# A hybrid decoder block on one core: state-space outputs turned round and double-buffered, q, k, v moved behind them, attention with its scores one block ahead

## The chip, the cores and the metric

The kernel runs on one core of a Trainium2 chip, as one program. The metric is device time in microseconds (us), the median of several executions; lower is better. The engines are named as in the profile: PE is TensorE (matmuls; PEld is its weight load, one for each matmul), DVE is VectorE, ACT is ScalarE, POOL is GpSimd, and SP is the engine that issues most of the DMAs. "q" behind a name (SPq, ACTq) is that engine's instruction queue. PEclk is the clock that TensorE was granted, as a share of its full 2.4 GHz; there are two levels, 1.0 and 0.5.

## The reference

One layer over 512 tokens of width 2048, all in float32:

```python
h = modulate(rmsnorm(x, g_mix), shift1, scale1)          # shift, scale, gate: silu(c) @ w_ada + b_ada
q, k, v, u, gate_logits = split(h @ w_in + b_in)         # 1024 + 256 + 256 + 1024 + 2 * 2048 columns
y_attn = sliding_window_attention(rope(q), rope(k), v, sinks) @ w_attn_branch
y_ssm = s5_ssm(u, ...) @ w_ssm_branch
merged = sigmoid(gate0) * y_attn + sigmoid(gate1) * y_ssm
x = x + gate1 * (merged @ w_out)
x = x + gate2 * peer(modulate(rmsnorm(x, g_ffn), shift2, scale2), ...)   # product-key experts
return rmsnorm(x, g_final)
```

Attention has 16 query heads over 4 key heads, a window of 128 and blocks of 128 tokens. The state-space branch has 64 groups of 16 channels with 64 complex states each: a scan over time, outputs `C x + D u`, then gelu and a gated linear unit. The change touches the layer from the u projection to the attention branch; the expert part behind it, which takes the larger half of the time, is as before.

## The kernel before

Activations lie channel-major (128 channels by 512 tokens a tile). A large product keeps float32 accuracy by splitting both factors into a rounded part and a rest and adding three matmuls (`product`, L201 to L203). One **projection** is 128 output channels over 2048 inputs: 48 matmuls of 512 columns, two weight loads of 512 KB on SP's queue, a cast on ACT (L185) and a subtraction on DVE (L187) for each. `w_in` has 52 projections: 8 for u in the head, and 44 others, of which 12 are q, k and v and 32 are gate logits. Each projection of gate logits also issues two pieces of the adaLN product, each a 512 KB load and one DVE instruction (L140).

The order is this. **Head** (L408 to L466): the first adaLN columns, the norm, and the eight u projections in five cuts of the contraction. In the second and third cut (c of 1 and 2) the rest of the weights is taken on POOL (L437). POOL also prepares the state-space part there: constants, powers (L356) and the rotation tables `rc`, `rs` (L372 to L380, doubling from 1 to 64 columns in six steps), which SP then stores (L527 to L529).

**State-space slices** (`ssm_slice`, L545 to L674): eight slices of eight groups. A slice has four steps: (1) POOL forms the tables `mt`, `cl_r`, `cl_i`; (2) PE transposes `mt` (L581), forms the small kernel `km` (L590, L591), which goes through DRAM and comes back as `intra` (L598 to L602), and turns u (L613); (3) PE forms the chunk inputs (L623), and DVE rotates them, scans over 64 chunks and rotates back (L629 to L652); (4) PE forms the outputs (L661 to L663): for each of eight groups three products of a 128-column stationary table with 64 moving columns, x being the moving side. ACT copies them out and they go to `y_d` in pieces of 64 elements. Between the steps the loop takes one projection from `dense()` at a time: 16 in all here, the 12 of q, k, v first. Most tiles of a slice have one buffer.

**Attention** (`attend`, L688 to L733): 16 blocks, four query blocks by four key heads, query block outermost. Each has scores (L699), a masked softmax on DVE, ACT and POOL, four or eight transposes (L721) and the product with v (L726). One projection follows in program order after the first half of each block, 16 in all. The 12 that are left run behind it (L739). Then come the attention branch (`w_ab`, L764), with the gelu of `y_d` on ACT beside it (L759 to L762), the gated linear unit, and the rest.

Program order is not the order on the chip. The framework plans every engine's instruction order ahead of time on a simulated timeline (L1300): of the instructions that are ready there it takes the earliest in the program; weight loads have a head start (L172). On the chip each engine, and SP's queue, then keeps that order and waits where an operand is late. `issue_after(ins)` plans a block's instructions of that engine behind `ins`. Every fp32 matmul outside `product` shows as two rows in the trace.

Of the kernel before, what the change touches and what calls it, by code (L numbers as in the profile page):

```python
# [18 lines left out]
TT = 4  # L19
# [40 lines left out]
def hybrid_block(tc, I, out, dbg=None):  # L60
# [311 lines left out]
    nc.gpsimd.memset(rc[:, :, 0:1], 1.0)  # L372
    nc.gpsimd.memset(rs[:, :, 0:1], 0.0)
    w = 1
    while w < 64:
        ub, vb = (z[:, :, None].to_broadcast([128, PAIRS, w]) for z in (ur, ui))
        cmul(rc[:, :, w:2 * w], rs[:, :, w:2 * w], rc[:, :, 0:w], rs[:, :, 0:w], ub, vb, ra[:, :, 0:w])
        cmul(vr, vi, ur, ui, ur, ui, t0)
        ur, ui, vr, vi = vr, vi, ur, ui
        w *= 2  # L380
# [49 lines left out]
    def head_product(c):  # L430
        k0, n = HEAD_CUTS[c]
        if c == 0:
            head.extend(mm_tile() if i % 2 else aux_tile() for i in range(8))
        for i in range(8):
            h, l = split_weights(I["w_in"][12 + i][k0 // 8][:, k0 % 8 * 128:(k0 % 8 + n) * 128], n,
                                 nc.gpsimd.tensor_tensor if c in (1, 2) else tt)
            for k in range(n):  # L437
                kk = k0 + k
                nc.tensor.matmul(head[i], h[:, k], h_hi[:, kk], start=(kk == 0), stop=False)
                nc.tensor.matmul(head[i], h[:, k], h_lo[:, kk], start=False, stop=False)  # L440
                nc.tensor.matmul(head[i], l[:, k], h_hi[:, kk], start=False, stop=(kk == KT - 1))
            yield
# [15 lines left out]
    y_d = dr.tile([1024, 8, 64], F32, name="y_d")  # L458
# [8 lines left out]

    ap_ = pool("ap", "left")
    qr = ap_.tile([128, 8, T], F32, name="qr")
    kr = ap_.tile([128, 2, T], F32, name="kr")  # L470
    vv = ap_.tile([128, TT, 256], F32, name="vv")
    rp = pool("rp", "left")
    rcos = rp.tile([128, T], F32, name="rcos")
    rsin = rp.tile([128, T], F32, name="rsin")
    posi = tmp.tile([128, T], I32, name="t0", tag="t0")
    ang = row("ev")
    nc.sync.dma_start(posi, I["positions"][None, :].to_broadcast([128, T]))
    nc.vector.tensor_copy(ang, posi)
    ts(ang, ang, freq, None, op0=OP.mult)
    reduce_angle(ang, rcos)  # L480
    sin_cos(rsin, rcos, ang)
    ts(rsin, rsin, sgn, None, op0=OP.mult)
# [22 lines left out]
    def dense():  # L505
        jobs = [(8 + i, rope, kr[:, i]) for i in range(2)]
        jobs += [(10 + i, value, vv[:, :, i * 128:(i + 1) * 128]) for i in range(2)]
        jobs += [(i, rope, qr[:, i]) for i in range(8)]
        last = None
        for m, finish, dst in jobs:  # L510
            o = projected(m)
            if last:
                last[0](*last[1:])
            last = finish, dst, o
            yield
        for i in range(32):
            o = projected(20 + i, 1)
            nc.scalar.dma_start(sg_d[i], o)
            if last:
                last[0](*last[1:])  # L520
                last = None
            yield

    dense_work = dense()


    with tc.issue_after(loads[-1]):  # L527
        for i, t_ in enumerate((rc, rs)):
            nc.sync.dma_start(rot_d[:, :, i], t_.rearrange("p (a b) c -> p a b c", a=8))  # L529
# [5 lines left out]
    with tc.issue_after(loads[-1]):  # L535
        nc.sync.dma_start(bass.AP(tensor=km_d.tensor, offset=km_d[0].offset + 128, ap=[[240, 128], [30720, 8], [1, 112]]),
                            zero[:, None, :].to_broadcast([128, 8, 112]))
# [7 lines left out]
    def ssm_slice(s):  # L545
# [21 lines left out]
        cl_r, cl_i = tl("cl_r", [128, 4, 16, 8]), tl("cl_i", [128, 4, 16, 8])  # L567
# [9 lines left out]
        for mt, name in zip(mts, ("mi_r", "mi_i")):  # L577
            dst = tl(name, [128, 4, 128])
# [20 lines left out]
        iraw, intra = tl("iraw", [128, 8, 128]), tl("intra", [128, 8, 16, 8])  # L599
# [3 lines left out]
        rot = tl("rot", [128, 2, 256])  # L603
# [6 lines left out]
        u = tl("uc", [128, 8, 64])  # L610
# [3 lines left out]
        uj = tl("uj", [128, 8, 64])  # L614
# [12 lines left out]
        ta = tl("t2", [128, 512])[:, 0:256]  # L627
        w_r, w_i = (tl("mt", [128, 4, 16, 8], 2).rearrange("p a h j -> p (a h j)")[:, 0:256] for _ in range(2))
# [11 lines left out]
        x_r, x_i = tl("x_r", [128, 4, 64]), tl("x_i", [128, 4, 64])  # L640
# [13 lines left out]
        y = tl("uc", [128, 8, 64])  # L654
        for two in range(2):
            p = aux_tile()
            rows = slice(two * 64, two * 64 + 64)
            for a in range(4):
                g = 2 * a + two
                o = p[:, a * 64:(a + 1) * 64]  # L660
                nc.tensor.matmul(o, cl_r[rows, a].rearrange("p h j -> p (h j)"), x_r[rows, a], start=True, stop=False)  # L661
                nc.tensor.matmul(o, cl_i[rows, a].rearrange("p h j -> p (h j)"), x_i[rows, a], start=False, stop=False)
                nc.tensor.matmul(o, intra[:, 4 * two + a].rearrange("p h j -> p (h j)"), uj[:, g], start=False, stop=True)  # L663
            nc.scalar.copy(y[:, two::2], p[:, 0:256].rearrange("p (a c) -> p a c", a=4))
        nc.scalar.dma_start(chunked_ap(y_d), y)

    slices = [ssm_slice(s) for s in range(8)]
    next(slices[0])
    for s in range(8):
        for _ in slices[s]:  # L670
            next(dense_work)
        if s < 7:
            next(slices[s + 1])
    close(ss)  # L674
    close(sp)
    close(rp)
# [11 lines left out]
    def attend(b, n):  # L688
# [7 lines left out]
        for r2 in range(2):  # L696
            p = aux_tile().rearrange("p (a c) -> p a c", a=2)
            for r in range(2):
                nc.tensor.matmul(p[:, r, 0:wd], qr[rows, np_ * 4 + r2 * 2 + r, b * 128:(b + 1) * 128],  # L699
                                 kr[rows, np_, k0:k0 + wd], start=True, stop=True)  # L700
            stt(sv[:, 2 * r2:2 * r2 + 2], p[:, :, 0:wd], 0.125, mk[:, None, :].to_broadcast([128, 2, wd]),
                op0=OP.mult, op1=OP.add)
# [11 lines left out]
        yield  # L714
# [3 lines left out]
        for kc in range(nk):  # L718
            p = aux_tile()
            for r in range(4):  # L720
                nc.tensor.transpose(p[:, r * 128:(r + 1) * 128], sc[:, r, kc * 128:(kc + 1) * 128], ident)  # L721
            pt = aw.tile([128, 512], F32, name="pt", tag="pt", bufs=3)
            nc.scalar.copy(pt, p)
            pts.append(pt)
# [5 lines left out]
    for b in range(TT):  # L730
        for n in range(4):
            for _ in attend(b, n):
                next(dense_work)  # L733
    close(aw)
    close(ap_)
# [495 lines left out]

def shape_constants():
# [17 lines left out]
def device_inputs(x):  # L1250
# [5 lines left out]
    b_in = np.concatenate([l["b_in"][:1024][qo], l["b_in"][1024:]])  # L1256
    d = {
# [8 lines left out]
                                                     l["b_glu"])], axis=1),  # L1266
# [3 lines left out]
        "w_sb": chunked(l["w_ssm_branch"]),  # L1270
        "w_glu": chunked(l["w_glu"]),
# [33 lines left out]
```

## Time and profile before

| | us |
|---|---|
| median of 3 runs | 3866.27 (3858.65 to 3869.51) |
| profiled execution, its own time | 3862.01 |
| its span, first to last instruction | 3860.2 |
| mean granted clock of TensorE | 0.953 |

| stretch of the span, us | what runs |
|---|---|
| 0 to 206 | head |
| 206 to 558 | eight state-space slices, 16 projections and the start of the next |
| 558 to 901 | attention blocks, and projections |
| 901 to 931 | the last projections of gate logits |
| 931 to 1021 | attention branch |
| 1021 to 3860 | gated linear unit, merge, output product, experts, last norm |

A row of the timeline has the start, the time taken, the engine, the line and the operation, out<-in, the shape, how many were merged, and in brackets how long the engine sat idle before it and what released it. A row of the waits says who waited for whom, in total us, how many times, and the longest. A row of the stretches has each engine's busy time (and instructions), the granted clock, the share of the DMA engines and GB/s. A busy PE need not be at its peak, since matmuls overlap.

### The profile page before, as it was taken

The numbers are of one execution on the slowest core, as the hardware profiler recorded it, in microseconds if no ns is written. First come the engines' busy times: TensorE is split into PE (matmuls) and PEld (weight loads), VectorE is DVE, ScalarE is ACT, GpSimd is POOL, SyncE is SP. The second block draws the span as 40 slices with busy tenths as digits, with TensorE's granted clock in tenths as the row PEclk, the third lists the DMA queues.
The fourth block names the chain that finished last, engine by engine and source line by source line (L and its number), as shares of the span: only waits on it lengthen the run. The fifth ranks groups of instructions, "written<-read, shape, count | busy, mean of one in ns | idle before, by whom it ended". The sixth has DMA issues, their size and how long they took to land.

```text
span 3860.2 us, 51341 instructions
## 1 busy us (share of the span) xinstructions
PE 3572.5 (93%) x20045; PEld 3242.9 (84%) x20045; DVE 2757.2 (71%) x3948; ACT 1295.9 (34%) x1790; POOL 1006.0 (26%) x851
## 2 busy tenths in 40 slices
PE   7699999999999988887399999999999999998997
PEld 3477777777788888787389999999999999998997
DVE  7644445556863389999887888888867888857844
ACT  3232223334443332345323223333333233333323
POOL 7644520010000245255322212222202122212102
PEclk8889889999999999999599999999999999999999
DMA  8543345447954322267788899999976999958943
GB/s 294 195 154 87 115 147 178 166 161 290 330 168 161 126 64 74 83 245 289 270 324 327 337 336 348 345 343 353 347 251 246 334 342 344 340 179 290 327 128 113
DMA packets 274104, 921.60 MB, mean 239 GB/s; under 512 B 35394, under 2 KB 92866, under 8 KB 229956
## 3 DMA queue, kind: packets, MB, share of 16 engines
q1 hardware_dynamic: 204260, 533.91, 39.8%
q0 software_dynamic: 50048, 344.55, 24.5%
q10 hardware_dynamic: 19552, 39.85, 2.7%
q8 instruction: 157, 2.57, 0.3%
q14 instruction: 87, 0.71, 0.1%
HBM read 871.03 MB, written 47.12 MB: 238 GB/s over the span
## 4 chain that ended last, share of the span: by engine, by line
PE 64%; DVE 13%; issue 10%; DMA 7%; POOL 2%; ACT 1%; DVEq 0%; POOLq 0%; SPq 0%; ACTq 0%
PE mm L203 13%; PE mm L201 13%; PE mm L202 13%; PE aux L1187 6%; PE aux L1186 6%; PE aux L1185 6%; DVE wlo L187 2%; DMA rows<-in_up_rows,pick 1%; DMA rows<-in_down_rows,pick 1%; DMA gt<-g_d 1%; DMA raw<-in_up 1%; DVE rows L1016 1%; POOL rows L1010 1%; DVE cand L932 1%; DVE o L1089 1%
## 5 line engine op out<-in xcount | busy, mean ns | idle before, releaser
L185 ACT CAST whi<-raw 128x1024 fp32r<-128x1024 f32 (+2 forms) x744 | 759.3, 1022 | 1736.1 <-PE mm L202 811.2
L187 DVE TENSOR_TENSOR wlo<-raw,whi 128x1024 fp32r<-128x1024 f32 (+2 forms) x696 | 868.2, 1248 | 435.4 <-ACT whi L185 403.8
L203 PE MATMUL mm<-h_hi,wlo 128*128 128x352 f32 (+1 forms) x2752 | 955.5, 347 | 41.8 <-DVE wlo L187 41.6
L201 PE MATMUL mm<-h_hi,whi 128*128 128x352 f32 (+1 forms) x2752 | 952.2, 346 | 8.1 <-ACT whi L185 8.1
L202 PE MATMUL mm<-h_lo,whi 128*128 128x352 f32 (+1 forms) x2752 | 949.1, 345 | 0.0
L1185 PE MATMUL aux<-wh,whi 128*128 128x352 f32 x2048 | 667.7, 326 | 39.4 <-ACT wh L191 22.4
L1187 PE MATMUL aux<-wh,wlo 128*128 128x352 f32 x2048 | 669.8, 328 | 27.2 <-DVE wlo L187 27.1
L1186 PE MATMUL aux<-wl,whi 128*128 128x352 f32 x2048 | 667.9, 326 | 2.3 <-DVE wl L192 2.3
L203 PEld LDWEIGHTS mm<-h_hi,wlo 128*128 128x128 f32 x2752 | 525.9, 191 | 79.8 <-DVE wlo L187 50.1
L201 PEld LDWEIGHTS mm<-h_hi,whi 128*128 128x128 f32 x2752 | 525.7, 191 | 40.6 <-ACT whi L185 9.7
L202 PEld LDWEIGHTS mm<-h_lo,whi 128*128 128x128 f32 x2752 | 527.1, 192 | 32.0 <-issue 4.4
L1185 PEld LDWEIGHTS aux<-wh,whi 128*128 128x128 f32 x2048 | 390.7, 191 | 45.9 <-ACT whi L185 23.3
L1187 PEld LDWEIGHTS aux<-wh,wlo 128*128 128x128 f32 x2048 | 390.4, 191 | 35.1 <-DVE wlo L187 34.7
L1186 PEld LDWEIGHTS aux<-wl,whi 128*128 128x128 f32 x2048 | 390.3, 191 | 3.4 <-DVE wl L192 3.4
L1016 DVE SCALAR_TENSOR_TENSOR rows<-rows,hrow 128x2048 f32<-128x2048 f32 x160 | 370.3, 2316 | 18.8 <-DMA rows<-in_down_rows,pick 18.2
L140 DVE SCALAR_TENSOR_TENSOR adaw<-adaw,cb 128x1024 f32<-128x1024 f32 x176 | 227.3, 1298 | 146.5 <-DMA adaw<-in_w_ada 146.4
L1010 POOL DMA_INDIRECT rows<-in_up_rows,pick x128 | 151.7, 1185 | 577.2 <-DVE rows L1016 479.3
L1027 DVE SCALAR_TENSOR_TENSOR yrow<-rows,fit,yrow 128x2048 f32<-128x2048 f32 x127 | 297.8, 2345 | 4.1 <-DMA rows<-in_up_rows,pick 4.1
L1010 POOL DMA_INDIRECT rows<-in_down_rows,pick x128 | 151.8, 1186 | 525.4 <-DVE yrow L1027 291.6
L1188 DVE SCALAR_TENSOR_TENSOR x<-aux,mod,x 128x352 f32<-128x352 f32 x256 | 148.6, 581 | 181.2 <-PE aux L1187 180.8
L213 POOL TENSOR_TENSOR rstd<-rstd,t 128x512 f32<-128x512 f32 (+2 forms) x42 | 50.7, 1207 | 661.7 <-ACT t L211 661.0
L187 POOL TENSOR_TENSOR wlo<-raw,whi 128x1024 fp32r<-128x1024 f32 (+1 forms) x48 | 105.9, 2211 | 115.4 <-ACT whi L185 114.0
(431 smaller groups left out, 4696.1 us busy)
## 6 DMA issues: line engine op xcount, KB each, us to landing
raw<-in_down SPq DMA_DIRECT2D x256, 512.0 KB
raw<-in_up SPq DMA_DIRECT2D x256, 512.0 KB
adaw<-in_w_ada SPq DMA_DIRECT2D x192, 512.0 KB
raw<-in_w_in SPq DMA_DIRECT2D x88, 512.0 KB
g_d<-stg ACTq DMA_DIRECT2D x22, 1024.0 KB
gt<-g_d SPq DMA_DIRECT2D x16, 1408.0 KB
raw<-in_w_out SPq DMA_DIRECT2D x32, 512.0 KB
raw<-in_w_query SPq DMA_DIRECT2D x32, 512.0 KB
```

Source lines behind the costliest of these rows:

```text
L140: stt(w, w, 1.0, cb[:, half], op0=OP.mult, op1=OP.mult, accum_out=part[:, half:half + 1])
L185: nc.scalar.copy(h, r)
L187: sub(l, r, h.bitcast(F32), op=OP.subtract)
L201: nc.tensor.matmul(p, h[:, k], (xh[kk] if isinstance(xh, list) else xh[:, kk]), start=first, stop=False)
L202: nc.tensor.matmul(p, h[:, k], (xl[kk] if isinstance(xl, list) else xl[:, kk]), start=False, stop=False)
L203: nc.tensor.matmul(p, l[:, k], (xh[kk] if isinstance(xh, list) else xh[:, kk]), start=False, stop=last)
L1010: nc.gpsimd.indirect_dma_start(out=r.rearrange("p k c -> p (k c)"), out_offset=None, in_=I[table], in_offset=bass.IndirectOffsetOnAxis(ap= ...
L1016: stt(r, r, 1.0, hrow, op0=OP.mult, op1=OP.mult, accum_out=f[:, n:n + 1])
L1027: stt(y, r, f[:, n:n + 1], y, op0=OP.mult, op1=OP.add)
L1185: nc.tensor.matmul(p, h[:, j], WH[j], start=(j == 0), stop=False)
L1186: nc.tensor.matmul(p, h[:, j], WL[j], start=False, stop=False)
L1187: nc.tensor.matmul(p, l[:, j], WH[j], start=False, stop=(j == GI - 1))
```

## The change

Six edits, of which the last three only follow from the others.

- The rotation tables become a function, called on POOL behind the last POOL subtraction of the head's third cut; their stores, and a clear of `km_d`, move from SP's queue to POOL's.
- The slices come first, with the projections of gate logits 0 to 15 between their steps. Most tiles of a slice get two buffers (`w_r`, `w_i` their own), and step 1 runs two slices ahead, step 2 one.
- Outputs are turned round: x and u are stationary (64 columns), the tables move (128 columns). Two groups share the 128 output rows, one in each half. ACT copies, 16 small products with the identity turn the result back, ACT applies gelu, and `y_d` is stored as rows of 512.
- q, k, v are grouped by pairs of key heads. Seven of their projections run between the slices and attention.
- Attention has the key head outermost. Scores of the next block are issued first, then one or two projections whose PE work is planned behind those scores, then the rest of the block; the 21 projections that are left all lie there. `pt` has two buffers instead of three.
- `z` is loaded straight from `y_d`; the rows of `w_glu`, `w_ssm_branch` and `b_glu` are put in the new channel order on the host.

```diff
-    loads = []
+    loads, subs = [], []
...
-        sub(l, r, h.bitcast(F32), op=OP.subtract)
+        subs.append(sub(l, r, h.bitcast(F32), op=OP.subtract).ins)
...
+    def rotations(ur, ui, vr, vi):
...
+        for i, t_ in enumerate((rc, rs)):
+            nc.gpsimd.dma_start(rot_d[:, :, i], t_.rearrange("p (a b) c -> p a b c", a=8))
...
+            if c == 2 and i == 7:
+
+                with tc.issue_after(subs[-1]):
+                    rotations(ur, ui, vr, vi)
             yield
...
+    dense_work = gate_logits(range(16))
...
+        cl_r, cl_i = tl("cl_r", [128, 4, 16, 8], 2), tl("cl_i", [128, 4, 16, 8], 2)
...
+        p = aux_tile()
+        for a in range(4):
+            for n_ in range(3):
+                for two in range(2):
+                    rows = slice(two * 64, two * 64 + 64)
+                    o = p[rows, a * 128:(a + 1) * 128]
+                    if n_ < 2:
+                        x_, cl_ = ((x_r, cl_r), (x_i, cl_i))[n_]
+                        nc.tensor.matmul(o, x_[rows, a], cl_[rows, a].rearrange("p h j -> p (h j)"), start=(n_ == 0), stop=False)
+                    else:
+                        nc.tensor.matmul(o, uj[:, 2 * a + two], intra[:, 4 * two + a].rearrange("p h j -> p (h j)"),
+                                         start=False, stop=True)
+        y = tl("y", [128, 8, 64])
+        nc.scalar.copy(y, p.rearrange("p (m j) -> p j m", j=8))
+        p = aux_tile()
+        for j in range(8):
+            for two in range(2):
+                rows = slice(two * 64, two * 64 + 64)
+                nc.tensor.matmul(p[rows, j * 64:(j + 1) * 64], y[rows, j], ident[rows, rows], start=True, stop=True)
+        zs = tl("zs", [128, T])
+        act(zs.rearrange("p (c j) -> p c j", j=8), p.rearrange("p (j c) -> p c j", j=8)[:, :, ::-1], AF.Gelu_apprx_tanh)
+        nc.scalar.dma_start(y_d[s], zs)
+
+    slices = [ssm_slice(s) for s in range(8)]
+    for s, n in ((0, 2), (1, 1)):
+        for _ in range(n):
+            next(slices[s])
+    for s in range(8):
+        next(slices[s])
+        next(dense_work)
+        if s < 7:
+            next(slices[s + 1])
+        next(slices[s], None)
+        if s < 6:
+            next(slices[s + 2])
+        next(dense_work)
+    close(ss)
+    close(sp)
...
+    jobs = [(8, rope, kr[:, 0]), (10, value, vv[:, :, 0:128])] + [(i, rope, qr[:, i]) for i in range(4)]
+    jobs += [(9, rope, kr[:, 1]), (11, value, vv[:, :, 128:256])] + [(i, rope, qr[:, i]) for i in range(4, 8)]
...
+    dense_work = heads()
+    for _ in range(7):
+        next(dense_work)
...
-        yield
+        yield scored
...
-    for b in range(TT):
-        for n in range(4):
-            for _ in attend(b, n):
-                next(dense_work)
+
+    blocks = [attend(b, n) for n in range(4) for b in range(TT)]
+    next(blocks[0])
+    for i, block in enumerate(blocks):
+        with tc.issue_after(next(blocks[i + 1])) if i + 1 < len(blocks) else contextlib.nullcontext():
+            for _ in range(2 if i < 5 else 1):
+                next(dense_work, None)
+        next(block, None)
...
     for k in range(8):
-        y = row("ev")
-        nc.sync.dma_start(y, y_d[k * 128:(k + 1) * 128].rearrange("p j c -> p (j c)"))
-        act(z[:, k].rearrange("p (c j) -> p c j", j=8), y.rearrange("p (j c) -> p c j", j=8)[:, :, ::-1], AF.Gelu_apprx_tanh)
+        nc.sync.dma_start(z[:, k], y_d[k])
```

## Rows read from the trace of the kernel before

**Rows 1.** The page: each engine's busy time, its share of the span, its instructions.

```profile
PE 3572.5 (93%) x20045; PEld 3242.9 (84%) x20045; DVE 2757.2 (71%) x3948; ACT 1295.9 (34%) x1790; POOL 1006.0 (26%) x851
```

**Rows 2.** Stretches of the span: busy time by engine, granted clock, DMA share, GB/s.

```profile
104.00:131.60 27.60, 0.00 (x0) 0.00 (x0) 5.53 (x11) 0.00 (x0) 27.60 (x37) 0.56 0.11 39
131.60:206.00 74.40, 69.40 (x280) 53.70 (x280) 52.53 (x80) 29.26 (x50) 29.81 (x20) 0.96 0.72 242
206.00:558.00 352.00, 341.69 (x1811) 269.96 (x1810) 162.46 (x290) 92.87 (x115) 168.29 (x186) 0.87 0.41 123
558.00:901.00 343.00, 343.00 (x1476) 260.26 (x1477) 186.39 (x297) 123.72 (x264) 32.03 (x16) 0.99 0.47 167
901.00:931.00 30.00, 30.00 (x134) 24.83 (x133) 20.57 (x34) 6.46 (x8) 0.00 (x0) 1.00 0.88 336
```

**Rows 3.** Waits of 95 to 206 us, the engines'.

```profile
PE aux L441 <- POOL wlo L187: 29.1, 2, 28.5
```

**Rows 4.** Waits of 95 to 206 us, those of SP's queue.

```profile
SPq L183 <- POOL vr L344: 27.5, 1, 27.5
```

**Rows 5.** Timeline of POOL, parts of 75 to 213 us.

```profile
75.11 1.25 POOL L342 TENSOR_TENSOR rc<-rc,vr 128x32 f32<-128x32 f32 x1
...
127.82 0.25 POOL L345 TENSOR_TENSOR vi<-cs,sn 128x32 f32<-128x32 f32 x1
...
140.80 1.30 POOL L347 TENSOR_TENSOR vi<-vi,pt 128x32 f32<-128x32 f32 x1
...
178.69 2.15 POOL L187 TENSOR_TENSOR wlo<-raw,whi 128x512 fp32r<-128x512 f32 x1 [1.47 <-ACT whi L185]
212.60 0.35 POOL L543 MEMSET bd<- 128x128 f32 x2 [31.76 <-DMA rot_d<-rs]
```

**Rows 6.** Timeline of PE, the outputs of one slice (matmuls of projections between left out).

```profile
423.62 0.44 PE L661 MATMUL aux<-x_r,cl_r 64*128 64x64 f32 x4
425.58 0.43 PE L662 MATMUL aux<-x_i,cl_i 64*128 64x64 f32 x2
...
426.31 0.43 PE L661 MATMUL aux<-x_r,cl_r 64*128 64x64 f32 x2
426.58 0.38 PE L662 MATMUL aux<-x_i,cl_i 64*128 64x64 f32 x2
426.89 0.43 PE L663 MATMUL aux<-uj,intra 128*128 128x64 f32 x2
427.26 0.43 PE L661 MATMUL aux<-x_r,cl_r 64*128 64x64 f32 x2
...
430.98 0.69 PE L661 MATMUL aux<-x_r,cl_r 64*128 64x64 f32 x2
...
432.64 0.69 PE L661 MATMUL aux<-x_r,cl_r 64*128 64x64 f32 x2
...
435.82 1.91 PE L581 MATMUL aux<-cst,mt 128*128 128x128 f32 x8
```

**Rows 7.** A stretch of the same slice, columns as in rows 2.

```profile
428.20:438.40 10.20, 10.20 (x40) 8.94 (x40) 3.86 (x4) 1.92 (x4) 7.60 (x8) 0.51 0.38 126
```

**Rows 8.** Timeline of PE: other small products, and a change between kinds of work.

```profile
401.46 0.14 PEld L590 LDWEIGHTS aux<-cl_r,bd 128*32 128x32 f32 x2 [0.35 <-issue]
...
409.04 0.69 PE L623 MATMUL aux<-uc,mi_r 128*64 128x64 f32 x16
...
578.27 1.16 PE L699 MATMUL aux<-kr,qr 64*128 64x128 f32 x8
```

**Rows 9.** Waits of 206 to 558 us, the engines'.

```profile
ACT intra L602 <- DMA iraw<-km_d: 52.2, 8, 10.9
```

**Rows 10.** PE's matmuls of L203, one third of the projections' matmuls, in one stretch.

```profile
558.00:901.00 343.00, 155.41 (x393) 74.37 (x393) 0.99 0.47 167
```

**Rows 11.** Timeline around the end of the last attention block.

```profile
890.07 1.03 PE L721 MATMUL aux<-cst,sc 128*128 128x128 f32 x8
...
895.58 1.07 PE L726 MATMUL aux<-pt,vv 128*64 128x512 f32 x2
```

More of the change, by code (lines that the diff above doesn't have):

```diff
@@ L1 @@
+import contextlib
 import numpy as np
@@ L371, in hybrid_block @@
         ur, ui, vr, vi = vr, vi, ur, ui
[L372 to L380, printed above, removed]
+    def rotations(ur, ui, vr, vi):
+        nc.gpsimd.memset(rc[:, :, 0:1], 1.0)
+        nc.gpsimd.memset(rs[:, :, 0:1], 0.0)
+        w = 1
+        while w < 64:
+            ub, vb = (z[:, :, None].to_broadcast([128, PAIRS, w]) for z in (ur, ui))
+            cmul(rc[:, :, w:2 * w], rs[:, :, w:2 * w], rc[:, :, 0:w], rs[:, :, 0:w], ub, vb, ra[:, :, 0:w])
+            cmul(vr, vi, ur, ui, ur, ui, t0)
+            ur, ui, vr, vi = vr, vi, ur, ui
+            w *= 2
+        for i, t_ in enumerate((rc, rs)):
+            nc.gpsimd.dma_start(rot_d[:, :, i], t_.rearrange("p (a b) c -> p a b c", a=8))
     hp = pool("hp", "left")
@@ L503, in value, with gate_logits @@
         nc.scalar.copy(dst, p.rearrange("p (b c) -> p b c", b=TT))
[L505 to L514, printed above, removed]
-            yield
-        for i in range(32):
+    def gate_logits(ids):
+        for i in ids:
             o = projected(20 + i, 1)
             nc.scalar.dma_start(sg_d[i], o)
-            if last:
-                last[0](*last[1:])
-                last = None
             yield
[L524 to L529, printed above, removed]
+    dense_work = gate_logits(range(16))
     close(st0)
@@ L534, in hybrid_block @@
     nc.gpsimd.memset(zero, 0.0)
-    with tc.issue_after(loads[-1]):
-        nc.sync.dma_start(bass.AP(tensor=km_d.tensor, offset=km_d[0].offset + 128, ap=[[240, 128], [30720, 8], [1, 112]]),
-                            zero[:, None, :].to_broadcast([128, 8, 112]))
+    nc.gpsimd.dma_start(bass.AP(tensor=km_d.tensor, offset=km_d[0].offset + 128, ap=[[240, 128], [30720, 8], [1, 112]]),
+                        zero[:, None, :].to_broadcast([128, 8, 112]))
     diag = ss.tile([32, 16], F32, name="diag")
@@ L598, in ssm_slice @@
         nc.gpsimd.dma_start(bass.AP(tensor=km_d.tensor, offset=km_d[s].offset, ap=[[960, 32], [240, 4], [1, 128]]), km)
-        iraw, intra = tl("iraw", [128, 8, 128]), tl("intra", [128, 8, 16, 8])
+        iraw, intra = tl("iraw", [128, 8, 128]), tl("intra", [128, 8, 16, 8], 2)
         nc.gpsimd.dma_start(iraw, bass.AP(tensor=km_d.tensor, offset=km_d[s].offset,
@@ L625, in ssm_slice @@
             pv.append(p[:, 0:256])
-        ta = tl("t2", [128, 512])[:, 0:256]
-        w_r, w_i = (tl("mt", [128, 4, 16, 8], 2).rearrange("p a h j -> p (a h j)")[:, 0:256] for _ in range(2))
+        ta, w_r, w_i = (tl(n_, [128, 256]) for n_ in ("ta", "w_r", "w_i"))
         tt(w_r, pv[0], rcos_, op=OP.mult)
@@ L653, in ssm_slice @@
         yield
[L654 to L664, printed above, removed]
@@ L675, in hybrid_block @@
     close(sp)
-    close(rp)
+    ap_ = pool("ap", "left")
+    qr = ap_.tile([128, 8, T], F32, name="qr")
+    kr = ap_.tile([128, 2, T], F32, name="kr")
+    vv = ap_.tile([128, TT, 256], F32, name="vv")
+    rp = pool("rp", "left")
+    rcos = rp.tile([128, T], F32, name="rcos")
+    rsin = rp.tile([128, T], F32, name="rsin")
+    posi = tmp.tile([128, T], I32, name="t0", tag="t0")
+    ang = row("ev")
+    nc.sync.dma_start(posi, I["positions"][None, :].to_broadcast([128, T]))
+    nc.vector.tensor_copy(ang, posi)
@@ new lines, in hybrid_block, with heads @@
+    ts(ang, ang, freq, None, op0=OP.mult)
+    reduce_angle(ang, rcos)
+    sin_cos(rsin, rcos, ang)
+    ts(rsin, rsin, sgn, None, op0=OP.mult)
+    jobs = [(8, rope, kr[:, 0]), (10, value, vv[:, :, 0:128])] + [(i, rope, qr[:, i]) for i in range(4)]
+    jobs += [(9, rope, kr[:, 1]), (11, value, vv[:, :, 128:256])] + [(i, rope, qr[:, i]) for i in range(4, 8)]
+    def heads():
+        last = None
+        for m, finish_, dst in jobs:
+            o = projected(m)
+            if last:
+                last[0](*last[1:])
+            last = finish_, dst, o
+            yield
+        gates = gate_logits(range(16, 32))
+        next(gates)
+        last[0](*last[1:])
+        yield
+        yield from gates
@@ L698, in attend @@
             for r in range(2):
-                nc.tensor.matmul(p[:, r, 0:wd], qr[rows, np_ * 4 + r2 * 2 + r, b * 128:(b + 1) * 128],
-                                 kr[rows, np_, k0:k0 + wd], start=True, stop=True)
+                scored = nc.tensor.matmul(p[:, r, 0:wd], qr[rows, np_ * 4 + r2 * 2 + r, b * 128:(b + 1) * 128],
+                                          kr[rows, np_, k0:k0 + wd], start=True, stop=True).ins
             stt(sv[:, 2 * r2:2 * r2 + 2], p[:, :, 0:wd], 0.125, mk[:, None, :].to_broadcast([128, 2, wd]),
@@ L728, in attend @@
         split(hi, lo, po[rows].rearrange("p (r q) -> p r q", r=4))
-    for b in range(TT):
-        for n in range(4):
-            for _ in attend(b, n):
-                next(dense_work)
+    blocks = [attend(b, n) for n in range(4) for b in range(TT)]
[5 more added lines that the diff above has]
+        next(block, None)
     close(aw)
+    close(rp)
     close(ap_)
```

43 lines of the change are left out of this document (13 added, 30 removed).

## The prediction

> **What bounds the kernel now.** I read the page first: the reader sees PE busy for 93% of the span [rows 1], so time can only come from stretches where PE stands still, runs at its lower clock, or does work that can be made smaller. Then the stretches [rows 2], for where that is. The changed part ends with the last projection at about 931 us; of what follows, everything keeps its instructions, so I move it as a block. Ahead of 931 the reader finds three different stretches. From 104 to 131.6 PE, its weight load and ACT have no instruction at all, and POOL is busy throughout. From 206 to 558 PE is busy, but its mean clock is 0.87. From 558 to 901 PE is busy 343.0 of 343.0 at 0.99: nothing there can be gained by hiding waits, only by removing work, and the change removes none of attention's.
>
> The waits then say why PE stood still. PE waited 28.5 us at a stretch for a subtraction on POOL [rows 3], and SP's queue 27.5 for the same POOL work [rows 4]: the weight buffer that POOL had not yet freed held back the loads behind it, and the DMAs fell to 39 GB/s [rows 2]. The timeline of POOL shows what stood in front: the rotation tables, from 75.11 to 142.1 [rows 5].
>
> For the low clock I read one slice on PE's timeline [rows 6] and its clock [rows 7]. The outputs take 0.44 + (435.82 - 425.58) = 10.7 us. Three pairs of rows take 0.95 us at first (426.31 to 427.26) and 1.66 later (430.98 to 432.64), with the granted clock at its lower level, 1.2 GHz, from 428.2 to 438.4. Before the fall PE had done nothing but these small products for about 3 us. All eight triples would take 7.6 us at the upper level and 13.3 at the lower.
>
> **The change part by part.**
>
> *Rotations behind the head's POOL subtractions.* This removes the standstill: 27.6 us [rows 2]. Late next are the other fifteen subtractions, each fed by ACT's cast, in a stretch where PE is already busy 69.4 of 74.4 us, so nothing of like size is behind it. What moves: the last subtraction ends at 180.8 now, so at about 153 then, and the rotations follow. They took 142.1 - 75.1 = 67 us less three subtractions of about 1.3, so 63; they would end near 216, and their two stores, now issued on POOL behind them and no longer by SP among weight loads, have to land before step 1 of the first slice starts: say 220 (an estimate from these), against 212.6 now [rows 5]. So PE is 28 us earlier and the slices are, if anything, later. The cover is the projections of gate logits: one is 48 matmuls at 30.0/134 us [rows 2], 10.75 us, and 16 of them are to be had; from PE's 178 to the first slice products (220 plus 21 us of POOL's step 1) five or six are needed. Without that cover the gain is nil. I take -27.6, bounds 0 and -28.5.
>
> *Outputs turned round.* Out: 48 rows a slice at 10.7 us. In: 48 rows with 64 stationary and 128 moving columns, 32 small rows with the identity, and one more visit by PE. The trace has no such product. The nearest from below is L623, also 64 stationary columns and the two output halves in turn: 16 rows of 64 columns in 0.69 us, 0.043 each; at double the columns 0.086, and 48 make 4.1. From above it is L699, 128 moving columns over 64 rows: 8 in 1.16 us, 0.145 each, 48 make 7.0 [rows 8]. I take 5.0, nearer to L623, which has the same alternation. The identity products have L623's very size: 32 x 0.043 = 1.4 (from above 4.6). A visit costs an idle 0.35 on the way in [rows 8], 0.5 with the way back. Sum 6.9 a slice (6.0 to 12.1), against 10.7: -3.8 x 8 = -30, bounds -38 and +11. ACT's two strided passes a slice run while PE has projections; ACT is busy 93 of 352 us there.
>
> The row also shows what a change between products over 64 and over 128 rows costs: L661 to L662 (both 64) 0.27 us, L662 to L663 (128) 0.31, back 0.37 [rows 6]. The Trainium skill (TensorEngine Tiling (Array Packing), Key Properties) says that changing the tiling mode drains TensorE, and the turned products change it twice in each of four groups of a slice. By the row's 0.04 to 0.10 that is under 1 us a slice and inside the 5.0; were each drain worth the 0.35 of a visit, the sum would lose 8 x 0.35 = 2.8 us a slice, 22 in all.
>
> *The clock.* If the turned outputs no longer bring it down, the rest of the slice gains too. In the stage 0.13 x 352 / 0.5 = 91 us ran at the lower level [rows 2], of which outputs 8 x 7.6 = 61 (428.2 to 435.82, [rows 6, 7]); the other 30 lose 15 us. The one slice I read gives 2.6 / 2 x 8 = 10. I take -13, bounds -15 and 0.
>
> *Slices double-buffered and ahead.* PE never waits long for a slice now, so this takes no wait off the path: 0. It must keep POOL ahead of a faster PE. POOL has 168.3 us in the stage, 21 a slice [rows 2], and the trip of `km` through DRAM makes ACT wait up to 10.9 [rows 9]. From 220, eight times 21 and a last slice of some 27 (trip, copy, outputs, gelu) end near 415, while PE, 71 us ahead of before, ends the stage near 487. Those 72 us are the cover. Moving q, k, v behind the slices moves their work and adds none; the adaLN pieces (DVE) move forward into a stage where DVE is busy 162 of 352.
>
> *Attention.* The same blocks and projections, on a PE without a gap: 0. "Held" projections cannot gain there, and the chain of a block lies under two of them. At the end it loses: before, projections covered the last block until 931; now `w_ab` follows. Exposed are eight transposes (1.03), a copy, two pairs with v (1.07 each, [rows 11]) and a cast and subtraction, about 5; the first products of `w_ab` read blocks long done. +4, bounds 0 and +6. The gelu that leaves ACT behind attention was beside matmuls: 0.
>
> **Sum**: -27.6 - 30 - 13 + 4 = -66.6. Against the profiled execution's own 3862.0: 3795. The median of the runs is 4.3 above that execution; I set 3797.
>
> **The rivals.**
>
> 1. *The clock still falls.* For: the turned products also leave half the array empty and come in bursts. Against: attention has bursts of L699 and L726 and stays at 0.99 [rows 2]. Then the outputs slow by the present ratio, 10.7/7.6: 6.9 becomes 9.7, a gain of 8 in all, and the clock's 13 is lost: -27.6 - 8 + 4 = -32, 3830.
>
> 2. *The standstill comes back at the first slice.* PE keeps its planned order, and if the plan puts slice 0 ahead of the projections, PE waits for POOL there: the 27.6 is given back, 3823. For: the present plan had PE meet POOL 28 us late [rows 3], and one and the same 128x32 operation takes POOL 0.25 or 1.30 us [rows 5]. Against: the wait for the stores at 212.6 held up no PE work. The Trainium skill (GPSIMD Engine Reference, Key points) says that GpSimd shares its SBUF interfaces with VectorE and contends with its instructions of two inputs; the spread of that row agrees, and DVE is busy 52.5 of the 74.4 us [rows 2] into which the rotations move.
>
> 3. *POOL becomes the bound, and the kernel is slower.* With gates used up early, each slice could wait for POOL's cycle: tables, `km`, the trip, two more stores. Attention and what lies before it need, back from 931: 21 x 10.75 = 226; attention's own 343 - 3 x 393 x 0.224 = 79 [rows 10]; 4; seven projections, 75; and ten products that rotate q and k, at L726's 1.07 some 10: 394. So slower begins where the slices end after 537, which is (537 - 220 - 27)/8 = 36 us a slice. At 42, the present (558 - 220)/8, it would be 220 + 8 x 42 + 27 = 583, +46: 3908. Against it stand POOL's 21.
>
> **How the numbers follow.** My forecast has 0.60, with its own range 3765 to 3825; rival 1 0.18, rival 2 0.12, both together (3858) 0.04, rival 3 0.06. The range 3755 to 3850 takes in the forecast with the bounds of the outputs and both single rivals. A difference under 0.3% (11.6 us) can't be told from none here: faster 0.88, same 0.05, slower 0.07.
>
> **What would show it.** Right: no stretch without PE instructions between 90 and 180; the u projections done near 178; clock above 0.95 from there to attention; turned outputs near 5 us a slice; the attention branch's first matmul near 865. Wrong: a wait of PE for POOL or for `intra` at the first slice (rival 2) or at most slices (rival 3), or half clock behind each output burst (rival 1). I would be quite wrong if PE went idle in attention, where I allow 4 us.

## The result, and the profile after

The kernel after takes 3823.44 us (median of 4 runs, 3811.51 to 3826.45) against 3867.89 of the kernel before: a ratio of 0.9887, 95% interval 0.9867 to 0.9907. That is 44 us where 67 were forecast. The profiled execution took 3821.48 us, its span 3819.7.

The page of the kernel after, engines (as in [rows 1]), and then its stretches (columns as in [rows 2]):

```profile
PE 3522.9 (92%) x20301; PEld 3191.8 (84%) x20301; DVE 2794.0 (73%) x3948; ACT 1273.6 (33%) x1771; POOL 1013.8 (27%) x854
```

```profile
104.00:131.60 27.60, 21.03 (x82) 16.44 (x80) 26.96 (x42) 9.41 (x15) 9.62 (x7) 0.88 0.95 350
...
226.00:480.00 254.00, 224.35 (x1795) 169.97 (x1794) 151.60 (x247) 74.17 (x93) 157.09 (x163) 0.97 0.45 145
480.00:560.00 80.00, 80.00 (x346) 64.09 (x344) 34.89 (x46) 21.71 (x25) 0.00 (x0) 1.00 0.28 96
560.00:890.00 330.00, 314.66 (x1334) 234.00 (x1335) 180.65 (x296) 113.32 (x251) 27.71 (x16) 0.99 0.42 154
```

The reader is to see three things beside [rows 2]. The first stretch, empty on PE before, is at work. The slices (226 to 480) run at 0.97 instead of 0.87, but PE is idle 29.7 us there, against 10.3 before. And attention (560 to 890), in which PE had been busy throughout, has 15.3 us of idle PE.

Everything up to the attention branch is what changed: its first matmul comes at 931.0 before and 890.2 after, and what follows takes 2929.2 and 2929.5. I call this first matmul **the mark**; the profiles of the experiments are compared by it. From 90 us to the mark, the time from each PE matmul to the next, summed by line, gives this account (a wait counts with the matmul ahead of it):

| from one matmul to the next, us | before | after | |
|---|---|---|---|
| u projections, with the standstill | 119.9 | 85.4 | -34.5 |
| outputs, identity products | 85.8 | 42.7 | -43.1 |
| transposes of attention | 11.0 | 29.1 | +18.1 |
| chunk inputs and turning of u | 17.6 | 30.4 | +12.8 |
| 44 projections (2112 matmuls in both) | 512.2 | 523.5 | +11.3 |
| the rest | 94.4 | 88.9 | -5.5 |
| sum | 840.9 | 800.0 | -40.9 |

The two gains are as large as forecast, or larger. The three losses had been priced at nothing. The wait behind the first of them stands in one row, PE's waits of 470 to 900 us (before, PE had none from 558 to 931):

```profile
PE aux L757 <- ACT pt L754: 15.3, 12, 1.8
```

The timeline shows one of the twelve:

```profile
591.49 0.60 PE L752 MATMUL aux<-cst,sc 128*128 128x128 f32 x4
...
593.23 0.60 ACT L754 COPY pt<-aux 128x512 f32<-128x512 f32 x1
593.88 1.07 PE L757 MATMUL aux<-pt,vv 128*64 128x512 f32 x2 [1.80 <-ACT pt L754]
594.88 2.97 PE L730 MATMUL aux<-kr,qr 64*128 64x256 f32 x8
```

Behind the transposes PE had nothing to do but the product with v, which waits for ACT's copy of them; only then come the next scores, and behind these the projections. In the kernel before, projections stand in this place: 20 to 24 of their matmuls in each of the 16 blocks, 22 in the first:

```profile
571.71 0.60 PE L721 MATMUL aux<-cst,sc 128*128 128x128 f32 x4
...
576.95 0.39 PE L203 MATMUL mm<-h_hi,wlo 128*128 128x512 f32 x1
577.27 1.07 PE L726 MATMUL aux<-pt,vv 128*64 128x512 f32 x2
```

Right behind this first of the twelve waits, from 595 to 603, the clock of the kernel after is at 0.57, which costs another 0.43 x 8 = 3.4 us; behind the other eleven it stays up.

```profile
595.00:603.00 8.00, 8.00 (x21) 5.90 (x22) 3.92 (x8) 2.74 (x10) 0.13 (x1) 0.57 0.14 53
```

The second loss is in the slices. First DVE's waits for adaLN pieces, before (206 to 558) and after (178 to 480), and then DVE's group of these pieces after, with PE's longest wait:

```profile
DVE adaw L140 <- DMA adaw<-in_w_ada: 22.4, 10, 4.3
```

```profile
DVE adaw L142 <- DMA adaw<-in_w_ada: 52.9, 12, 10.6
```

```profile
L142 DVE SCALAR_TENSOR_TENSOR adaw<-adaw,cb 128x1024 f32<-128x1024 f32 x31 | 52.9, 1709 | 52.9 <-DMA adaw<-in_w_ada 52.9
```

```profile
PE aux L640 <- DVE x_r L626: 10.2, 4, 5.5
```

The gain of the outputs, one slice of the kernel after, answers to [rows 6]:

```profile
467.48 0.44 PE L640 MATMUL aux<-cl_r,x_r 64*64 64x128 f32 x4
467.75 0.39 PE L640 MATMUL aux<-cl_i,x_i 64*64 64x128 f32 x4
468.06 0.44 PE L642 MATMUL aux<-intra,uj 128*64 128x128 f32 x4
468.43 0.44 PE L640 MATMUL aux<-cl_r,x_r 64*64 64x128 f32 x4
...
470.61 0.39 PE L640 MATMUL aux<-cl_i,x_i 64*64 64x128 f32 x4
```

Counted as in the account, the outputs take 3.8 to 4.5 us in seven of the slices and 5.8 in the first, which has a wait of about 2 in it; the identity products take 1.08.

### The profile page after: what moved, and what is told of

It reads as the page before. It is cut to its first block, busy times and chain, and to the rows that moved or that the text cites. A ratio compares the mean times of both kernels' runs of the same rounds, so it can differ in the third digit from the quotient of the medians.

```text
span 3819.7 us, 51844 instructions
## 1 busy us (share of the span) xinstructions
PE 3522.9 (92%) x20301; PEld 3191.8 (84%) x20301; DVE 2794.0 (73%) x3948; ACT 1273.6 (33%) x1771; POOL 1013.8 (27%) x854
## 5 line engine op out<-in xcount | busy, mean ns | idle before, releaser
L203 PE MATMUL mm<-h_hi,whi 128*128 128x352 f32 (+1 forms) x2752 | 954.7, 347 | 6.4 <-ACT whi L187 6.3
L203 PEld LDWEIGHTS mm<-h_hi,whi 128*128 128x128 f32 x2752 | 525.8, 191 | 51.4 <-issue 16.1
L142 DVE SCALAR_TENSOR_TENSOR adaw<-adaw,cb 128x1024 f32<-128x1024 f32 x176 | 235.8, 1347 | 86.1 <-DMA adaw<-in_w_ada 85.9
```

The costliest lines, as they stand in the source:

```text
L142: stt(w, w, 1.0, cb[:, half], op0=OP.mult, op1=OP.mult, accum_out=part[:, half:half + 1])
L203: nc.tensor.matmul(p, h[:, k], (xh[kk] if isinstance(xh, list) else xh[:, kk]), start=first, stop=False)
```

## The experiments

Eleven kernels were timed. The ratios are to the kernel before, run beside each on the same chip; that of the kernel after is 0.9887, and differences of two ratios carry both intervals. The mark is that of one profiled execution. Where I speak of PE's **longer waits**, they are the steps of over 0.9 us from one matmul to the next, less 0.3 each, from the last u projection to the last product of the slices: 10.2 us (4 of them) before, 35.6 (19) after.

| | ratio, 95% | mark, us |
|---|---|---|
| 1 after, nothing held | 0.9815 (0.9793 to 0.9838) | 870.9 |
| 2 before + rotations late | 0.9941 (0.9918 to 0.9965) | 921.8 |
| 3 before + outputs turned | 0.9863 (0.9840 to 0.9887) | 888.0 |
| 4 after, pieces late | 0.9841 (0.9822 to 0.9861) | 871.8 |
| 5 = 1 + 4 | 0.9806 (0.9786 to 0.9825) | 851.3 |
| 6 = 2 + 3 | 0.9869 (0.9845 to 0.9893) | 871.7, then a wait |
| 7 = 5, slices single | 0.9782 (0.9760 to 0.9805) | 851.7 |
| 8 after, halves in turn | 0.9910 (0.9887 to 0.9932) | 901.6 |
| 9 after, rotations early | 0.9957 (0.9941 to 0.9972) | 910.2 |
| 10 = 7, rotations early | 0.9832 (0.9811 to 0.9852) | 875.5 |
| 11 = 1, slices single | 0.9789 (0.9774 to 0.9805) | 862.4 |

**1. Nothing held in attention.**

```diff
-        with tc.issue_after(next(blocks[i + 1])) if i + 1 < len(blocks) else contextlib.nullcontext():
-            for _ in range(2 if i < 5 else 1):
-                next(dense_work, None)
+        if i + 1 < len(blocks):
+            next(blocks[i + 1])
+        for _ in range(2 if i < 5 else 1):
+            next(dense_work, None)
```

> The kernel after, with the projections of attention no longer planned behind the next block's scores; everything else the same. In the kernel after, PE waits 15.3 us, 12 times, between a block's transposes and its product with v, for ACT's copy. Theory (the hold causes it: nothing may be planned into that gap): the wait falls below 3 us, projections stand between transposes and product as before the change, and the time falls by 13 to 16 us, to 3808 (3804 to 3813), ratio to the kernel before 0.985. Rival (the wait is needed cover: projections used up earlier leave the last blocks bare): the stretches without a projection move to the end of attention, the last product with v is followed by more than 5 us without PE work, and the time stays within 4 us of 3823, ratio 0.988 to 0.990.

3797.33 us, 0.72% +- 0.30 below the kernel after: 28 us. That is more than the 13 to 16 expected, with a wide interval. The mark comes 19.3 us earlier, which is the 15.3 of waits and the 3.4 of the clock. PE's only wait from 560 to 890 and its stretches are now:

```profile
PE mm L203 <- ACT at_hi L193: 0.7, 1, 0.7
```

```profile
560.00:610.00 50.00, 50.00 (x217) 38.56 (x217) 23.65 (x38) 19.14 (x43) 3.52 (x3) 1.00 0.26 89
610.00:850.00 240.00, 240.00 (x1037) 179.39 (x1036) 141.70 (x226) 86.78 (x193) 21.46 (x13) 1.00 0.46 165
```

And the same block, with projections in the gap:

```profile
594.15 0.60 PE L752 MATMUL aux<-cst,sc 128*128 128x128 f32 x4
...
600.51 0.39 PE L205 MATMUL mm<-h_hi,wlo 128*128 128x512 f32 x1
600.83 1.07 PE L757 MATMUL aux<-pt,vv 128*64 128x512 f32 x2
```

The theory holds, the rival falls: the hold made the wait.

**2. Rotations alone, on the kernel before.**

```diff
-    while w < 64:
...
+            if c == 2 and i == 7:
+                with tc.issue_after(subs[-1]):
+                    rotations(ur, ui, vr, vi)
```

> The kernel before, with one part of the change: the rotation tables are formed on POOL behind the last of its subtractions in the head, and their stores go to POOL's queue. Theory (step 1 of the prediction): the 27.6 us in which PE had no instruction go, the projections cover the later tables, and the time falls by 24 to 30 us, to 3840, ratio 0.993. Rival 2 of the prediction (the standstill comes back at the first slice): PE waits 20 us or more at the first slice's transposes or chunk inputs, and the time stays within 5 us of 3868, ratio 0.999 to 1.001.

3840.38 us, -0.59% +- 0.24, 23 us. The u projections end at 178.9 instead of 206.9, 28.0 earlier; in the profiled execution, one of the slowest of its seven, only 9.2 of these reach the mark. PE's longer waits sum to 24.6 us and the outputs take 94.8 us instead of 85.8, so part of the gain is lost there. The theory holds in time, with a warning that I took up in 6, 9 and 10.

**3. Outputs alone, on the kernel before** (the outputs' code of the change, y and the gelu's result in existing buffers).

> The kernel before, with one part of the change: the outputs turned round (x and u stationary, identity products, gelu in the slice, y_d as rows); slices one behind another with single buffers, q, k, v and attention as before. Theory (the outputs are worth what the two rows say: 42.7 us of PE after, 85.8 before, the clock in both included): the time falls by 38 to 46 us, to 3826, ratio 0.989; the granted clock stays above 0.93 in the stage of the slices. Rival (a part of it turns into waits whatever the order of the slices: with less work of PE between the steps, PE waits for DVE, ACT and POOL): PE's waits in the stage rise by 15 us or more, and the time falls by 15 to 28 us, to 3846, ratio 0.994. A gain under 10 us would say that the outputs were no part of the bound.

3812.51 us, a gain of 53 (44 to 62), more than expected; the mark comes 43.0 earlier, as expected. Its slices, against [rows 2]:

```profile
206.00:523.00 317.00, 298.61 (x2085) 223.11 (x2085) 166.64 (x289) 98.02 (x118) 178.48 (x186) 0.97 0.44 137
```

The clock goes from 0.87 to 0.97 by the outputs alone, and PE's longer waits come to 16.7 us. This one part is worth as much as the whole change.

**4. adaLN pieces out of the slices' stage.**

```diff
-            o = projected(20 + i, 1)
+            o = projected(20 + i, 0 if i < 16 else 2 if i < 20 else 1)
...
-            o = projected(m)
+            o = projected(m, 1)
```

> The kernel after, with the 32 adaLN pieces of the 16 projections in the slices' stage moved out of it: two to each of the 12 projections of q, k and v, eight more to the first four projections of gate logits behind them. The work is the same in all. In the kernel after DVE waits 55.7 us for such pieces in the stage (13 times, up to 10.6), and PE has 16 gaps of together 33 us between 236 and 456 us, against 12 us in the kernel before. Theory (the pieces stand at the head of DVE's queue, waiting for their loads, in front of the slices' rotations and the weights' subtractions): PE's gaps in the stage fall below 18 us and the time falls by 13 to 22 us, to 3806, ratio 0.984. Rival (the gaps come from the order of the slices' own steps, or from POOL): the gaps stay above 26 us, the time stays within 5 us of 3823, ratio 0.988 to 0.990; if the pieces press on attention instead, it is over 3828.

3801.2 us; the mark comes 18.4 earlier. DVE's group of the pieces, 178 to 495 us:

```profile
L142 DVE SCALAR_TENSOR_TENSOR adaw<-adaw,cb 128x1024 f32<-128x1024 f32 x9 | 11.0, 1224 | 18.0 <-DMA adaw<-in_w_ada 18.0
```

Fewer pieces (9 for 31), less waiting (18.0 for 52.9), and each one shorter (1.22 us for 1.71). PE's longer waits fell to 22.7 rather than below 18, and attention kept its own. PE's waits for DVE, 22.5 us in the kernel after (174 to 480), are down to one, and the largest left are for ACT:

```profile
PE aux L559 <- ACT zs L652: 8.6, 3, 4.0
PE aux L642 <- ACT intra L580: 7.6, 1, 7.6
...
PE aux L640 <- DVE x_r L626: 1.0, 1, 1.0
```

The theory holds in time (0.46% +- 0.28, 18 us). But the edit did more than the theory says: POOL's rotation tables end at 195.3 instead of 200.5, and the first slice's products come at 217.8 instead of 226.4. How the price divides between the waiting in DVE's queue and this isn't shown.

**5. Both repairs.**

> The kernel after with both edits of the first round: nothing held in attention, and the adaLN pieces of the slices' stage moved to the projections of q, k and v. Theory (two separate losses, one in each stage): they add up, 3823 - 26 - 22 = 3775 (3765 to 3786), ratio to the kernel before 0.976; PE's gaps over 0.9 us below 25 us in the slices' stage and none from the first score to the attention branch. Rival (one loss seen twice: what is won in the slices is waited for in attention, where the pieces now stand at the head of DVE's queue): no better than 3790, ratio over 0.981, and PE's gaps come back in attention.

3787.53 us. By the mark the two add up (39 us earlier than after: 19.3 + 18.4 = 37.7); PE's longer waits are 21.3 us in the slices, and 1.9 in attention. By the time they do not: 0.9806 is 0.81% +- 0.28 below the kernel after, 31 us, and no clear step below 0.9815. Neither expectation was met cleanly; 11 returns to it.

**6. Rotations and outputs alone.**

> The kernel before with two parts of the change alone: rotations behind the head's subtractions, and outputs turned round; slices, q, k, v and attention as before. Theory (these two carry the whole gain, and the other four edits cost): ratio 0.9941 x 0.9863 = 0.9805, 3787 (3775 to 3800), below the kernel after. Rival (they need the second buffers and the steps ahead: PE, 28 us earlier and with less to do, waits for the slices): PE's gaps in the stage of the slices over 40 us and a time of 3810 to 3825, no better than the kernel after or than the outputs alone, ratio 0.985 to 0.990.

3808.47 us: by the time no better than the outputs alone (+0.06% +- 0.34). The rival's size came out, and its place in part: PE's longer waits are 32.0 us, not over 40, but 15 more than the 16.7 of 3. The mark comes 16.3 us before that of 3, and another 9.2 are lost behind it, in PE's waits of 870 to 895 us and on the timeline:

```profile
PE aux L736 <- POOL sc L728: 9.2, 1, 9.2
```

```profile
877.23 0.40 PE L203 MATMUL mm<-at_hi,wlo 128*128 128x512 f32 x1
886.78 1.54 PE L736 MATMUL aux<-cst,sc 128*128 128x128 f32 x6 [9.15 <-POOL sc L728]
```

PE, early and with less to do, had taken 946 projection matmuls by the end of the slices, where the kernel before had taken 802; the last blocks of attention then had no projection beside them, and PE stood before the last softmax. So of the 30 us by which the u projections end earlier than in 3, some 24 are waited off, more of them in the slices than at the end.

**7. Slices single again**, with both repairs.

```diff
-        cl_r, cl_i = tl("cl_r", [128, 4, 16, 8], 2), tl("cl_i", [128, 4, 16, 8], 2)
+        cl_r, cl_i = tl("cl_r", [128, 4, 16, 8]), tl("cl_i", [128, 4, 16, 8])
...
+    next(slices[0])
+    for s in range(8):
+        for _ in slices[s]:
+            next(dense_work)
+        if s < 7:
+            next(slices[s + 1])
```

> The kernel of both repairs (nothing held, adaLN pieces late), with the slices' tiles in one buffer again and one slice behind another, as in the kernel before. Theory (prediction: the second buffers take no wait off the path): within 8 us of the kernel of both repairs, some 3775, ratio 0.974 to 0.978. Rival (with the turned outputs and an earlier PE the second buffers do carry): PE's gaps in the stage rise by 20 us or more, and the time is 3790 or above, ratio over 0.980.

3782.59 us, the mark 0.4 us from that of 5. The ratio, 0.9782, lies between the two expectations, next to the theory's, and 0.24% +- 0.30 below that of 5, which can't be told from none. With nothing held and the pieces late, the prediction's 0 for the second buffers holds.

**8. The halves of the outputs in turn.**

```diff
-            for n_ in range(3):
-                for two in range(2):
+            for two in range(2):
+                for n_ in range(3):
```

> The kernel after, with the two inner loops of the turned outputs changed about: all three products of one half of the output rows, then the three of the other half, where the kernel after alternates between the halves. Same products, same operands; a change between 64-row and 128-row products comes four times a group pair where it came twice. In the kernel after the 48 rows of a slice take 34.1/8 = 4.3 us, near the 4.1 that I worked out from the alternating chunk inputs (0.043 each for 64 columns). Theory (the alternation is what made that row the right neighbour: products in different halves run beside each other): without it a product costs what the scores' row says, 0.145 or more, and a slice's outputs take 7 us or more: 20 to 30 us in eight slices, partly beside waits, time 3835 to 3850. Rival (the small product is simply that fast): the rows stay within 0.5 us a slice of 4.3, the time within 5 us of 3823.

3827.64 us. In seven of eight slices the outputs now take 7.5 to 7.8 us (a wait of 2 in the first left out), at full clock, over the 7 expected; in the sixth they take 11.7, at a clock of 0.63. One at full clock:

```profile
475.25 0.43 PE L640 MATMUL aux<-cl_r,x_r 64*64 64x128 f32 x2
475.52 0.38 PE L640 MATMUL aux<-cl_i,x_i 64*64 64x128 f32 x2
475.83 0.43 PE L642 MATMUL aux<-intra,uj 128*64 128x128 f32 x2
476.19 0.43 PE L640 MATMUL aux<-cl_r,x_r 64*64 64x128 f32 x2
```

The theory holds for the rows, not for the time: it rose by only some 9 us (0.23% +- 0.30) where 12 to 27 were expected, and the mark by 11.4. The outputs take 67.1 us in place of 34.1, but PE's longer waits fell to 16.1: more than half of the loss replaces waits.

**9. Rotations early, in the kernel after.** The edit of 2, undone.

> The kernel after with one part undone: the rotation tables are formed on POOL in the head again, ahead of its subtractions, and SP stores them. Theory (step 1 of the prediction, -27.6): PE stands some 27 us before 135 us again, the u projections end near 206, and the time is 3823 + 20 to 30, 3848, ratio 0.9935 to 0.997. Rival (the first slice's products start at 226 us in the kernel after and at 229 in the kernel before, so the slices bound the stage and PE's earlier start is only waited off there): PE's gaps in the stage fall from 35 us to below 20 and the time rises by less than 12 us, to 3823 to 3835, ratio below 0.992.

3843.06 us, 0.70% +- 0.25 above the kernel after: 27 us. The mark comes 20.0 later, and the u projections end at 205.6 instead of 173.9. PE's longer waits fall to 22.4, so the rival's mechanism exists and takes some 13 us; but the time says theory.

**10. The same in the kernel of 7.**

> The fastest kernel so far (nothing held, adaLN pieces late, slices single and one behind another, ratio 0.978) with the rotations early again, as in the kernel before. Theory (where PE waits little in the slices, the head's 28 us are worth their whole size): the time rises by 20 to 30 us, to 3808, ratio 0.983 to 0.986. Rival (the slices' start is what counts, and it doesn't come earlier): it rises by less than 10 us, ratio 0.978 to 0.9805.

3795.59 us, 0.50% +- 0.30 above, 19 us; the mark 23.8 later. Theory again, a little under its size.

**11. Nothing held, slices single, pieces in the slices' stage.**

> The fastest kernel so far with the adaLN pieces back in the slices' stage, as in the kernel after: so nothing held, slices single and one behind another. Theory (the pieces cost 20 us by their waits in DVE's queue, whatever the slices' order): PE's gaps in the stage are over 27 us and the time is 12 to 22 us above 3782.6, ratio 0.981 to 0.984. Rival (they cost only where two slices share DVE's queue): gaps below 22 us and within 6 us of 3782.6, ratio 0.9765 to 0.980.

3777.49 us, the same as 7 within the interval: by the time, the rival. By the mark it is 10.7 later, and PE's longer waits are 23.5 us against 17.4 in 7, between the two. So the pieces' price is shown in the kernel after (18 us, by time and mark), and is smaller, or nothing that can be told, once one slice stands behind another. Against 1, which differs from it in the second buffers and the steps ahead alone, 11 has its mark 8.5 us earlier (0.26% +- 0.27 by the time), and longer waits of 23.5 us against 34.8. Why its time is as good as that of 7 isn't settled: in its profile the part behind the mark took 2913 us, where the other profiles have 2918 to 2932 for the same instructions.

## Why the prediction was right, and where its size failed

**Rotations, -27.6: right.** The u projections ended at 173.9 (forecast 178), undoing the part costs 27 us by time and 20 by the mark. POOL's tables ran from 147.9 to 200.5, 53 us where I had 63, and the first slice's products came at 226.4 against 228.7 before. The cover by gate logits was as described. What I had not said is that the gain hangs on what comes further down: on the kernel before with turned outputs none can be told by the time (6), because some 15 us are waited off in the slices and 9 at the end of attention, where the projections used early are missing.

**Outputs and clock, -43: the sum came out, its split did not, and that is in part luck.** The row of -43.1 in the account holds the outputs alone, for which I had -30: 4.3 us of outputs and 1.1 of identity products a slice, where I had 6.9 with a visit. Experiment 3's mark, 43.0 earlier, says the same, its rows of outputs giving 44.0. My other -13 was for the slices' other work at the lower clock. That work ran 34.5 us at the lower level before (206 to 558) and 23.3 after (174 to 480), so it won back some 6 us (half of the 11.2), and the longer waits, 10.2 us before and 35.6 after, took more than that. The neighbour chosen, the chunk inputs that alternate between the output halves, was the right one; without the alternation (8) the other bound, 7.0, was passed by half a microsecond or more. The clock kept 0.97. The Trainium skill's rule that a change of tiling mode drains TensorE (TensorEngine Tiling (Array Packing), Key Properties) was rightly not charged as a visit each: from a 64-row product to the 128-row one and back it is 468.06 - 467.75 = 0.31 and 0.37 us, as in [rows 6], and 8 has twice as many changes at the same steps.

**Attention's end, +4: wrong by 4.** The first matmul of the attention branch (890.22) comes right behind the last transposes (889.43, eight of them, 1.03 us); they and the last product with v stand among its matmuls.

**"Held" projections, 0: this step failed.** The prediction says that "held" projections cannot gain in attention, and concluded that nothing changes. It argued from a PE without a gap, which was so because projections stood in each wait for ACT's copy, 20 to 24 matmuls in all 16 blocks. The hold plans these behind the next scores, and in the order on the chip the scores come behind the product that waits. It costs 15.3 us of waits and 3.4 of clock; experiment 1 takes both away. I had named what would be "quite wrong", an idle PE in attention, but priced only the end of it.

**adaLN pieces moved forward, 0: this failed too.** I compared DVE's busy time (162 of 352) with the pieces. I left out where they stand: 16 more pieces in the stage, waiting for their loads in DVE's order with the slices' rotations and the weights' subtractions behind them, and many of them beside POOL's work, where they are slower (see the last section). They cost 18 us in the kernel after; that this is the waiting alone is argued, not shown.

**Second buffers, 0: right in the repaired kernel** (5 against 7), but under a wrong picture. With the pieces in the stage, as the change has them, 1 against 11 gives no gain either, and by the mark a loss of 8.5 us. I had PE never waiting long for a slice and 72 us of POOL's cover; PE, faster, then had its 19 longer waits, and 22.5 us of PE's waits from 170 to 480 were for DVE. The stage still ended at 480 (forecast 487), since the head and the outputs gave somewhat more than I took.

So the mark was forecast at 865 (931.0 less 66.6) and came at 890.2, 25 late. The hold makes 18.7 of these (15.3 + 3.4). The rest is the waits in the slices, less what the head gave beyond its term (34.5 for 27.6) and the 4 of attention's end. So two losses that the forecast had put at nothing, the hold and the waits in the slices, make most of the miss.

**The rivals.** 1, the clock still falls: no, 0.97. 2, the standstill comes back: its price, 3823, is the measured time, and still it is not the cause; no wait of 20 us stands at the first slice, and the head's gain is there when it is undone (9). Equal totals prove nothing about a mechanism. 3, POOL as the bound: no.

## What to carry to other kernels

An engine that is never idle shows that its order is well filled, not that the order may be changed at no cost: when a plan is pinned, look for the short waits that the free plan had filled. A stage's busy share says nothing of an instruction that waits for its load at the head of a queue: count what stands behind it. And a gain early in the program has to be followed to the end: work taken ahead as cover is missing later.

## What was not expected of the hardware

- The step from one small product to the next is the same 0.27, 0.31 and 0.37 us whether it is one product of 64 moving columns with 128 stationary ([rows 6], at the upper clock), one of 128 moving with 64 stationary (8), or two such in the two output halves (after). So the gain of the turned outputs at full clock lies in the second half riding along.
- Two bursts of the same length did not do the same to the clock. Experiment 8's outputs take about the 7.6 us worked out for before's at full clock, and kept it in seven of eight slices, where the kernel before lost it in all eight (0.51 to 0.88 in their stretches). The stretches of one slice of each, 8 and before:

```profile
380.10:388.30 8.20, 8.20 (x51) 5.04 (x50) 4.24 (x5) 0.00 (x0) 4.66 (x6) 1.00 0.50 106
```

```profile
382.10:393.30 11.20, 11.20 (x54) 9.27 (x54) 3.69 (x4) 2.01 (x3) 7.62 (x6) 0.74 0.33 106
```

The two differ in which side of the products is stationary, and in what runs around them; what of this matters was not tried.
- DVE and POOL are slower side by side. In the kernel after, from 178 to 480 us, the 14 adaLN instructions of DVE with no TENSOR_TENSOR of POOL beside them took 1.19 to 1.27 us, the other 17 took 2.11 in the mean and up to 3.42; the 9 of experiment 4 (178 to 495) all ran without POOL, at 1.22 or 1.23. In the kernel before, POOL's 128x32 product or sum took at most 0.32 us in the 50 cases in which neither a TENSOR_TENSOR nor a SCALAR_TENSOR_TENSOR of DVE ran beside it, and over 0.8 in 17 of the 55 in which one did. That is the spread of [rows 5].
